# Two neighbouring gate/up chunks as one product whose first half of K takes seven block products, in both feed-forwards of a macaron decoder block

## The chip, the cores and the metric

The kernel runs on one core of a Trainium2 chip. Time is device microseconds of one execution, as the median of several runs. TensorE is PE in the profile (PEld its weight loads), VectorE is DVE, ScalarE is ACT, GpSimd is POOL, and SP is the engine whose queue issues nearly all DMAs.

## The reference

The block reads 256 tokens of 1024 features (float32). Only its first and last stage, the two feed-forwards, are touched:

```python
def swiglu(x, w_gate, w_up, w_down):
    return (jax.nn.silu(x @ w_gate) * (x @ w_up)) @ w_down
...
h = h + 0.5 * swiglu(rmsnorm(h, ffn1_norm[l]), ffn1_w_gate[l], ffn1_w_up[l], ffn1_w_down[l])
...   # mixing: attention and chunked spatial gating, gated merge, output projection
h = h + 0.5 * swiglu(rmsnorm(h, ffn2_norm[l]), ffn2_w_gate[l], ffn2_w_up[l], ffn2_w_down[l])
return rmsnorm(h, final_norm)
```

`w_gate` and `w_up` are 1024 x 2816, `w_down` is 2816 x 1024.

## The kernel before, in words

**Three passes.** Each float32 product is made of fp32r products: every operand is kept as a high part (a rounded copy) and a low part (what the rounding left). `mm3` multiplies one 128-row block of K with 512 output columns in three matmuls (lines 240 to 242): high by high, high by low, low by high. A 128-token block of the activations is the stationary operand, 512 weight columns are the moving one.

**Chunks and units.** Gate and up are computed in eleven chunks of 256 hidden columns; a chunk has 256 gate and 256 up columns, that is 512 output columns for two token blocks and eight blocks of K, 8 x 2 x 3 = 48 matmuls into two PSUM banks (`chunk`). The weights of a chunk come in two units, one for each half of K, of four blocks each. A unit is fetched in two halves of 512 KB (`fetch_to`, ring `raw` of 7 buffers, SP queue). `split` turns each 128x1024 half into its parts: ACT writes the high one (line 245), DVE subtracts for the low one (line 247). Units live in the ring `w` of 5 buffers. `unit(i, ahead)` writes units up to `ahead` past the one that PE is about to use; in most of the feed-forwards `ahead` is DEEP = 4, so the next unit can be written as soon as PE has left the unit five places back.

**After a chunk** `Hidden.glu` scales by the token factors: ACT takes the SiLU of the gate columns out of PSUM (line 505), DVE multiplies with the up columns (507) and transposes 32x32 blocks (508). `Hidden.move` carries the result through DRAM (`f1way`, `f1back`) to the layout with hidden features on partitions, `f1h`.

**Seven products.** The down projections already take eight of their 22 blocks of K in pairs by a seven-product scheme (`seven`): a 2x2 arrangement of token blocks by K blocks times a 2x2 arrangement of K blocks by column halves in seven block products instead of eight. Four products use forms of the token side (four sums of 128x128 blocks, lines 543 to 546, then `split`), and four use sums of weight blocks, made on DVE by four adds of 128x512 (`quarters`, lines 194 to 197, tile `sum`, two buffers). The weights of such a pair are two units in the ring: "single" (three 512-column blocks used as they are) and "sums" (four made ones). Of the seven, three go straight into output banks, and four into shared banks (1, 5, 6 and 7), which `settle_seven` adds up at the end.

**Order.** PE and SP run in the order of the source. DVE and ACT are put in order by a scheduler, apart from the stretches under `in_order()`, which hold the start of the first feed-forward and all from its down projection to the second chunk of the second one. PSUM has eight banks. `n` is the normalised input in its two parts, `f` the chunks' banks, `accdown` and `acch` the banks of the two down projections, `h` the residual between the feed-forwards.

Of the kernel before, what the change touches and what calls it, by code (L numbers as in the profile page):

```python
# [43 lines left out]
REST = [k for k in range(FB) if k // 2 not in SEVEN]  # L44
PLAIN = len(REST) // 2
WARM = 17


@with_exitstack
def block_kernel(ctx, tc, t, out):  # L50
# [56 lines left out]
    def add_units(name, n):  # L107
        first = len(units)
        units.extend((name, i) for i in range(n))
        return first  # L110

    f1 = add_units("f1", 2 * NC)


    f1d = []
# [11 lines left out]
    mb = len(units)  # L129
    units.extend([("bg", 0), ("ba", 0), ("bg", 1), ("ba", 1)])  # L130
    mo = add_units("out", 4)
    f2 = add_units("f2", 2 * NC)

# [228 lines left out]
            banks[key] = bank(f"acc{name}" + "_".join(map(str, key)))  # L364
        mm3(banks[key], st, w, first, last)

    def seven(name, at, i, tokens_of, acc, shared, ahead=DEEP):


        a, b, d = tokens_of(2 * i, 0), tokens_of(2 * i + 1, 0), tokens_of(2 * i + 1, 1)  # L370
        last = i == SEVEN[-1]

        def of(w, n):
            return w[:, n, 0, :], w[:, n, 1, :]

        def form(n):
            return tuple(hidden.forms[i][:, n, two, :] for two in range(2))

        w = unit(at, ahead)
        product(shared, name, (1,), a, of(w, 0), last)  # L380
        product(acc, name, (0, 0), b, of(w, 1), False)
        product(acc, name, (0, 512), form(3), of(w, 2), False)
        w = unit(at + 1, ahead)
        product(shared, name, (5,), form(0), of(w, 0), last)
        product(shared, name, (7,), form(1), of(w, 1), last)
        product(shared, name, (6,), form(2), of(w, 2), last)
        product(acc, name, (1, 0), d, of(w, 3), False)
# [24 lines left out]
    def down(at, part_of, scale, hh, name, done, cuts, behind):  # L412

        acc, shared = {}, {}
        K = 2 * len(at)
        near = K - 4

        def add(ps, j, c0, n):
            sl = slice(c0, c0 + n)
            nc.vector.scalar_tensor_tensor(hh[:, j, sl], ps, scale, hh[:, j, sl], op0=ALU.mult, op1=ALU.add)

        def tokens_of(k, j):
            return tuple(p[:, j * P:(j + 1) * P] for p in part_of(k))

        def ends(j, c0, k):
            return k == (K - 1 if (c0, 512) in cuts[j] else near - 1)

        for i in range(len(at) - 2):
            if i in SEVEN:
                seven(name, at[i], i, tokens_of, acc, shared)
                if i == SEVEN[-1]:
                    settle_seven(name, shared, scale, hh)()
            else:
                w = unit(at[i], DEEP)
                for kk in range(2):
                    for j in range(NT):
                        for c0, n in HALVES:  # L440
                            product(acc, name, (j, c0), tokens_of(2 * i + kk, j),
                                    tuple(w[:, kk, two, c0:c0 + n] for two in range(2)), ends(j, c0, 2 * i + kk))
            for then in behind[i:i + 1]:
                then()
        for j in range(NT):
            for c0, n in HALVES:
                if (c0, n) not in cuts[j]:
                    add(acc[j, c0], j, c0, n)
        for j in range(NT):
            for hf, (c0, n) in enumerate(cuts[j]):  # L450
                whole = (c0, n) in HALVES
                ps = acc[j, c0] if whole else bank(f"end{name}{j}{c0}")[:, :n]
# [37 lines left out]
    class Hidden:  # L490
# [45 lines left out]
        def form(self, p, e, to):  # L536

            def of(j, k):
                return self.back[p][:, 4 * j:4 * j + 4, 64 * e + 32 * k:64 * e + 32 * (k + 1)]

            f = tmp.tile([P, 4, P], F32, tag="form", name=f"{self.name}form{p}{e}", bufs=1)
            of_f = [f[:, n].rearrange("p (q c) -> p q c", c=32) for n in range(4)]
            nc.vector.tensor_sub(of_f[0], of(1, 1), of(1, 0))
            nc.vector.tensor_sub(of_f[1], of(0, 0), of(1, 0))
            nc.vector.scalar_tensor_tensor(of_f[2], of_f[0], -1.0, of(0, 0), op0=ALU.mult, op1=ALU.subtract)
            nc.vector.tensor_add(of_f[3], of_f[2], of(0, 1))
            split(to[:, :, 0, :], to[:, :, 1, :], f)
            self.forms[2 * p + e] = to

        def settle(self, p):  # L550
# [65 lines left out]
    with in_order():  # L616
        x = inputs_of(front[:, KB:KB + KB * ROW])
        split_to(f1 + 3)
        for pair in range(KB // 2):
            square(x[:, 2 * pair:2 * pair + 2, :], pair, "1", "nC")  # L620
        split_half()
        token_sums("1")
        split_half()
        sum_parts("1")
        sums.append(chunk(f1, nT, "f1", 1))
        rs = token_factors("1")
        sums.append(chunk(f1, nT, "f1", 2))
        hidden = Hidden("f1")
        for c in range(2):
            hidden.glu(c, sums[c], rs)  # L630

    ht1 = act.tile([P, NT, D], F32, tag="nD", name="ht1")
    for j in range(NT):
        nc.sync.dma_start(ht1[:, j, :], t["by_tokens"][j * P:(j + 1) * P, :])
    for c in range(2, NC):
        if c > 2:
            sums.append(chunk(f1, nT, "f1", c, ahead=DEEP))
            hidden.form_behind(c, ("h", "nC"))
            for moved in (1, 2, 3) if c == 3 else (c,):
                hidden.move(moved)  # L640
        hidden.glu(c, sums[c], rs)
# [18 lines left out]
    with in_order():  # L660
# [30 lines left out]
        for n, (at, s) in enumerate(f1d):  # L691

            ahead = 1 if len(SEVEN) * 2 - 2 <= n < len(SEVEN) * 2 else DEEP
            if s is not None:
                seven("down1", at, SEVEN[s], tokens_of, acc, shared, ahead)
                if s == len(SEVEN) - 1:
                    settled.append(settle_seven("down1", shared, 0.5, ht1))
            else:
                w = unit(at, ahead)
                slots = range(4 * units[at][1], 4 * units[at][1] + 4)  # L700
                ends = slots[-1] == 2 * len(REST) - 1
                for slot, j in [(x, j) for j in range(NT) for x in slots] if ends else [(x, j) for x in slots for j in range(NT)]:
                    f, b = divmod(slot, len(REST))
                    last = b == len(REST) - 1
                    product(acc, "down1", (j, f * 512), tokens_of(REST[b], j),
                            tuple(w[:, slot % 4, two, :] for two in range(2)), last)
                    if last:
                        add(f, j, acc[j, f * 512])
                        if j == NT - 1:
                            from_way(h[:, f], h_way[f])  # L710
                            if f == 0:
                                settled.pop()()
            for then in rest[n:n + 1]:
                then()
            if n == len(f1d) - 3:
                norm_parts(0)
# [259 lines left out]
                nc.vector.transpose(squares32[:, b].rearrange("p (f c) r -> p f c r", f=2),  # L976
                                    h[:, :, b, :].rearrange("p f (c r) -> p f c r", r=32))
    hd = dram.tile([S, D], F32, name="hd")
    ht = act.tile([P, NT, D], F32, tag="nA", name="ht")
    for c in range(2, NC):  # L980
        ps = chunk(f2, nT3, "f2", c, ahead=DEEP)
        if c == 2:
            hidden.move(1)
        hidden.form_behind(c, ("h", "nB"))
        hidden.move(c)
        hidden.glu(c, ps, rs)
        if c == 3:
            for a in range(4):
                nc.sync.dma_start(hd[:, a * UC:(a + 1) * UC].rearrange("(b c) n -> c b n", c=32),
                                  squares32[32 * a:32 * a + 32].rearrange("p b k r -> p b (k r)"))  # L990
        elif c == 5:
            for j in range(NT):
                nc.sync.dma_start(ht[:, j, :], hd[j * P:(j + 1) * P, :])
        elif c == 7:
            gain4 = act.tile([P, D], F32, tag="ws", name="gain4")
            nc.sync.dma_start(gain4, t["final_norm"].to_broadcast([P, D]))

# [43 lines left out]
def _packed(inputs):  # L1041
# [33 lines left out]
    def chunks(w):  # L1075
# [6 lines left out]
    first = np.concatenate([columns(a["ffn1_norm"][0][order], KB), by_k.reshape(P, -1)], 1)  # L1082
    got = {
        "first": first,
        "f1": chunks(pairs[1]), "f2": chunks(pairs[2]),
        "by_tokens": a["x"][0][:, turned],
        "f1s": rows(down1)[list(SEVEN)],
        "f1d": down1.reshape(FB, P, 2, 512)[REST].transpose(2, 0, 1, 3).reshape(PLAIN, 4, P, 512).transpose(0, 2, 1, 3),
# [32 lines left out]
```

## Time and profile before

| | |
|---|---|
| median of 3 runs | 519.33 us (518.91 to 519.96) |
| the profiled execution: its own time, and its span | 519.43 us, 517.7 us |
| mean granted PE clock | 0.996 |
| PE, PEld, DVE, ACT, POOL busy | 509.5, 424.0, 403.9, 281.1, 12.0 us |
| PE instructions, DVE, ACT | 2377, 585, 395 |
| HBM read and written | 113.26 and 13.11 MB, 244 GB/s over the span |

The span runs from the first to the last instruction; the execution's own time has 1.7 us more around it. First feed-forward: gate and up chunks from 6 to 126 us, then its down projection to 185 us. Second one: chunks from 334 to 454 us, down projection to 510 us. A matmul's row says 389 ns, but that is from its start to its modelled end, and the next one starts before it. So rates are read from start times.

### The profile page before, as it was taken

Reading aid. Unit: us, or ns where it says so; the run is one execution under the profiler, and the core shown is the slowest. Engines: PE = TensorE matmul, PEld = TensorE weight load, DVE = VectorE, ACT = ScalarE, POOL = GpSimd, SP = SyncE. Lnnn points to the kernel's source line nnn. Section 1 sums busy time; section 2 is a strip of 40 time slices with the busy share of each in tenths; the row PEclk is TensorE's granted clock in tenths of the full one; section 3 lists DMA queues with packets and bytes.
Section 4 is the critical chain, followed back from the end, with each engine's and each line's share of the span. In section 5 each row is a group of like instructions: output and inputs, shape, how many; then the busy total and the mean of one; then the engine's idle time right before and its main releaser. Section 6 shows DMA issues by size and latency. Waiting matters only on the chain.

```text
span 517.7 us, 6795 instructions
## 1 busy us (share of the span) xinstructions
PE 509.5 (98%) x2377; PEld 424.0 (82%) x2377; DVE 403.9 (78%) x585; ACT 281.1 (54%) x395; POOL 12.0 (2%) x25
## 2 busy tenths in 40 slices
PE   8999999999999999999999999999999999999995
PEld 6888888888888888888888898888888888888884
DVE  5896685888798965579977776988876666899864
ACT  6775445455474736667565613668535544466702
POOL 0010000000000010000000000001000000000002
PEclk9999999999999999999999999999999999999998
DMA  8999499867576886796899665839989879389302
GB/s 312 359 335 392 142 316 329 263 181 256 163 226 221 270 311 214 186 325 239 204 361 333 240 184 161 304 98 307 310 255 325 249 282 282 91 282 282 124 0 82
DMA packets 63921, 126.81 MB, mean 245 GB/s; under 512 B 11664, under 2 KB 36752, under 8 KB 63760
## 3 DMA queue, kind: packets, MB, share of 16 engines
q1 hardware_dynamic: 63600, 126.06, 74.1%
q8 instruction: 18, 0.29, 0.2%
q10 hardware_dynamic: 288, 0.33, 0.2%
q14 instruction: 15, 0.12, 0.1%
HBM read 113.26 MB, written 13.11 MB: 244 GB/s over the span
## 4 chain that ended last, share of the span: by engine, by line
PE 94%; DMA 2%; DVE 1%; issue 1%; SPq 1%; ACT 0%; POOLq 0%; DVEq 0%; POOL 0%; ACTq 0%
PE f L242 15%; PE f L241 15%; PE f L240 15%; PE accdown L242 4%; PE accdown L241 4%; PE accdown L240 4%; PE acch L242 4%; PE acch L241 4%; PE acch L240 3%; PE acc L214 3%; PE g L241 3%; PE g L242 3%; PE g L240 3%; DMA raw<-in_gate 1%; PE acc L219 1%; DMA front<-in_first 1%
## 5 line engine op out<-in xcount | busy, mean ns | idle before, releaser
L247 DVE TENSOR_TENSOR w<-raw,w 128x1024 fp32r<-128x1024 f32 (+1 forms) x180 | 207.2, 1194 | 36.6 <-ACT w L245 36.1
L245 ACT CAST w<-raw 128x1024 fp32r<-128x1024 f32 (+1 forms) x180 | 176.3, 1030 | 52.1 <-PE f L242 38.5
L242 PE MATMUL f<-w,n 128*128 128x512 f32 x336 | 130.7, 389 | 0.0
L240 PE MATMUL f<-w,n 128*128 128x512 f32 x336 | 130.7, 389 | 0.0
L241 PE MATMUL f<-w,n 128*128 128x512 f32 x336 | 130.7, 389 | 0.0
L241 PEld LDWEIGHTS f<-w,n 128*128 128x128 f32 x336 | 63.1, 188 | 13.2
L240 PEld LDWEIGHTS f<-w,n 128*128 128x128 f32 x336 | 63.1, 188 | 13.1
L242 PEld LDWEIGHTS f<-w,n 128*128 128x128 f32 x336 | 63.1, 188 | 13.0
L505 ACT ACTIVATE f2s<-f,rstd 128x256 f32<-128x256 f32 x22 | 10.3, 474 | 30.1 <-PE f L242 30.1
L240 PE MATMUL accdown<-w,f1h 128*128 128x512 f32 x68 | 26.5, 389 | 0.0
L241 PE MATMUL accdown<-w,f1h 128*128 128x512 f32 x68 | 26.5, 389 | 0.0
L242 PE MATMUL accdown<-w,f1h 128*128 128x512 f32 x68 | 26.5, 389 | 0.0
L245 ACT CAST w<-sum 128x1024 fp32r<-128x1024 f32 x16 | 16.7, 1053 | 16.9 <-DVE sum L195 13.1
L240 PE MATMUL g<-w,n 128*128 128x512 f32 x64 | 24.9, 389 | 0.0
L241 PE MATMUL g<-w,n 128*128 128x512 f32 x64 | 24.9, 389 | 0.0
L240 PE MATMUL acch<-w,f2h 128*128 128x512 f32 x64 | 24.9, 389 | 0.0
L241 PE MATMUL acch<-w,f2h 128*128 128x512 f32 x64 | 24.9, 389 | 0.0
L242 PE MATMUL acch<-w,f2h 128*128 128x512 f32 x64 | 24.9, 389 | 0.0
L242 PE MATMUL g<-w,n 128*128 128x512 f32 x64 | 24.9, 389 | 0.0
L507 DVE SCALAR_TENSOR_TENSOR f2a<-f,rstd,f2s 128x256 f32<-128x256 f32 x22 | 10.2, 474 | 13.5 <-ACT f2s L505 13.5
L247 DVE TENSOR_TENSOR w<-sum,w 128x1024 fp32r<-128x1024 f32 x16 | 19.3, 1216 | 1.2 <-ACT w L245 1.2
L505 ACT ACTIVATE f1s<-f,rstd 128x256 f32<-128x256 f32 x22 | 10.2, 473 | 16.1 <-PE f L242 15.7
(225 smaller groups left out, 768.4 us busy)
## 6 DMA issues: line engine op xcount, KB each, us to landing
raw<-in_f SPq DMA_DIRECT2D x84, 512.0 KB, 6.2
raw<-in_f2d SPq DMA_DIRECT2D x22, 512.0 KB, 6.5
raw<-in_gate SPq DMA_DIRECT2D x16, 512.0 KB, 5.9
raw<-in_f1d SPq DMA_DIRECT2D x14, 512.0 KB, 5.0
raw<-in_f1s SPq DMA_DIRECT2D x8, 512.0 KB, 4.8
raw<-in_out SPq DMA_DIRECT2D x8, 512.0 KB, 5.4
f1way<-f1t SPq DMA_DIRECT2D x11, 256.0 KB, 5.6
f2way<-f2t SPq DMA_DIRECT2D x11, 256.0 KB, 6.1
```

The costliest lines, as they stand in the source:

```text
L214: nc.tensor.matmul(ps, st, both.rearrange("p two n -> p (two n)"), start=first, stop=last)
L219: nc.tensor.matmul(ps[:, n:], st, both[:, 0, :], start=False, stop=False)
L240: nc.tensor.matmul(ps, sh, mh, start=first, stop=False)
L241: nc.tensor.matmul(ps, sh, ml, start=False, stop=False)
L242: nc.tensor.matmul(ps, sl, mh, start=False, stop=last)
L245: nc.scalar.copy(hi, src)
L247: nc.vector.tensor_sub(lo, src, hi.bitcast(F32))
L505: nc.scalar.activation(sg, ps[j][:, :CH], AF.Silu, scale=rs[j])
L507: nc.vector.scalar_tensor_tensor(a, ps[j][:, CH:], rs[j], sg, op0=ALU.mult, op1=ALU.mult)
```

## The change

Chunks 6 and 7 of each feed-forward become one product of 1024 columns (2 x 512). Its first four blocks of K are taken in two pairs by `seven`, 2 x 7 x 3 = 42 matmuls where 2 x 8 x 3 = 48 stood; the last four blocks are multiplied as before (`rest`), first for chunk 6, then for chunk 7. Their weights are regrouped on the host: four units for the seven-product part (single, sums, single, sums) and one unit for each chunk's second half of K. The fetched bytes are the same.

```diff
+PAIR = {"f1": 6, "f2": 6}
...
+    def add_chunks(name):
+        c = PAIR[name]
+        first = add_units(name, 2 * c)
+        units.extend((f"{name}s2", i, what) for i in range(2) for what in ("single", "sums"))
+        units.extend((name, i) for i in range(2 * c, 2 * NC - 2))
+        return first
...
+    def make_forms(of, to, name):
+        f = tmp.tile([P, 4, P], F32, tag="form", name=name, bufs=1)
+        of_f = [f[:, n].rearrange("p (q c) -> p q c", c=32) for n in range(4)]
+        nc.vector.tensor_sub(of_f[0], of(1, 1), of(1, 0))
+        nc.vector.tensor_sub(of_f[1], of(0, 0), of(1, 0))
+        nc.vector.scalar_tensor_tensor(of_f[2], of_f[0], -1.0, of(0, 0), op0=ALU.mult, op1=ALU.subtract)
+        nc.vector.tensor_add(of_f[3], of_f[2], of(0, 1))
+        split(to[:, :, 0, :], to[:, :, 1, :], f)
+
+    def chunk_pair(name, at, nT, forms, ahead):
+        acc, shared = {}, {}
...
+        for i in range(2):
+            seven(name, at + 2 * i, i, tokens_of, acc, shared, forms[:, i], i == 1, ahead)
+        p1, p5, p6, p7 = (shared[n,] for n in (1, 5, 6, 7))
+        to = [sump.tile([P, NT, 512], F32, tag="sum", name=f"{name}{e}") for e in range(2)]
+        (c00, c10), (c01, c11) = ([x[:, j] for j in range(NT)] for x in to)
+        nc.scalar.copy(c00, p1)
+        nc.vector.tensor_add(c01, p6, c00)
+        nc.vector.tensor_add(c10, p7, c01)
+        nc.vector.tensor_add(c11, p5, c10)
+        nc.vector.tensor_add(c01, p5, c01)
+
+        def rest(e):
+            w = unit(at + 4 + e, ahead)
+            for k in range(4):
+                for j in range(NT):
+                    product(acc, name, (j, 512 * e), tokens_of(4 + k, j), (w[:, k, 0, :], w[:, k, 1, :]), k == 3)
+            for j in range(NT):
+                x = to[e][:, j]
+                (nc.vector.tensor_sub if e else nc.vector.tensor_add)(x, acc[j, 512 * e], x)
+            return [to[e][:, j] for j in range(NT)]
+        return rest
...
+        normed1 = sump.tile([P, 4, S // 32, 32], F32, tag="sum", name="normed1")
+        for k in range(4):
+            nc.scalar.activation(normed1[:, k].rearrange("p q c -> p (q c)"), x[:, k], AF.Identity, scale=front[:, k:k + 1])
...
-            sums.append(chunk(f1, nT, "f1", c, ahead=DEEP))
+            sums.append(chunk_of("f1", f1, nT, c, pair_forms))
+            if c == 3:
+                for i in range(2):
+                    make_forms(lambda j, k: normed1[:, 2 * i + k, 4 * j:4 * j + 4, :], pair_forms[:, i], f"pair1form{i}")
...
-    ht = act.tile([P, NT, D], F32, tag="nA", name="ht")
+    pair_forms = act.tile([P, 2, 4, 2, P], F32R, tag="nA", name="pairforms")
...
-        elif c == 5:
+        elif c == PAIR["f2"] + 2:
+            ht = act.tile([P, NT, D], F32, tag="nA", name="ht")
...
-        elif c == 7:
+        elif c == PAIR["f2"] + 3:
```

`chunk_of` sends c = 6 and 7 to the two calls of `rest`, c = 6 after `chunk_pair`; the second feed-forward gets the same lines as the first, with `normed` from `h`. The forms need the first four normalised blocks in plain float32, hence `normed1` and `normed`. In the second feed-forward the buffer `nA` first holds the forms, so the load of the residual `ht` moves from chunk 5 to chunk 8 and that of `gain4` from chunk 7 to chunk 9.

What the scheduler makes of it at three places follows. First DVE in the first feed-forward, while PE is in chunk 1. The tile `sq` holds the squares for the token factors, `sqp` their split sum, `w_270` the second unit of chunk 1, `w_285` (`w_290` after) the first of chunk 2. Before:

```order
L247 TENSOR_TENSOR w_270<-raw_0_192,w_270 128x2x512
L279 TENSOR_TENSOR sq_265<-sq_265 128x1024
L279 TENSOR_TENSOR sq_265<-sq_265 128x512
L279 TENSOR_TENSOR sq_265<-sq_265 128x256
L247 TENSOR_TENSOR w_270<-raw_1_194,w_270 128x2x512
L247 TENSOR_TENSOR sqp_280<-sq_265,sqp_280 128x256
L247 TENSOR_TENSOR w_285<-raw_0_196,w_285 128x2x512
```

After:

```order
L256 TENSOR_TENSOR w_270<-raw_0_192,w_270 128x2x512
L288 TENSOR_TENSOR sq_265<-sq_265 128x1024
L400 TENSOR_TENSOR pair1form_560<-normed_280 128x128
L288 TENSOR_TENSOR sq_265<-sq_265 128x512
L401 TENSOR_TENSOR pair1form_560<-normed_280 128x128
L288 TENSOR_TENSOR sq_265<-sq_265 128x256
L256 TENSOR_TENSOR w_270<-raw_1_194,w_270 128x2x512
L256 TENSOR_TENSOR sqp_285<-sq_265,sqp_285 128x256
L402 SCALAR_TENSOR_TENSOR pair1form_560<-pair1form_560,normed_280 128x128
L256 TENSOR_TENSOR w_290<-raw_0_196,w_290 128x2x512
```

The sums of the first forms now stand among the token sums, ahead of the second half of `w_270`.

Second, DVE at the end of the output projection, where `h` and the parts `n` for the second feed-forward are made and PE is about to begin its chunk 0; `w_2970` (`w_3021` after) is the first unit of chunk 1, `w_3013` (`w_3064`) its second. Before:

```order
L311 SCALAR_TENSOR_TENSOR n_2779<-h,cols,n_2779 128x256 x2
L247 TENSOR_TENSOR w_2970<-raw_0_2795,w_2970 128x2x512
L247 TENSOR_TENSOR w_2970<-raw_1_2836,w_2970 128x2x512
L279 TENSOR_TENSOR sq_2943<-sq_2943 128x1024
L279 TENSOR_TENSOR sq_2943<-sq_2943 128x512
L279 TENSOR_TENSOR sq_2943<-sq_2943 128x256
L247 TENSOR_TENSOR sqp_3007<-sq_2943,sqp_3007 128x256
L247 TENSOR_TENSOR w_3013<-raw_0_2840,w_3013 128x2x512
```

After:

```order
L401 TENSOR_TENSOR pairform_3414<-normed 128x128
L402 SCALAR_TENSOR_TENSOR pairform_3414<-pairform_3414,normed 128x128
L320 SCALAR_TENSOR_TENSOR n_2830<-h,cols,n_2830 128x256
L256 TENSOR_TENSOR w_3021<-raw_0_2846,w_3021 128x2x512
L256 TENSOR_TENSOR w_3021<-raw_1_2887,w_3021 128x2x512
L288 TENSOR_TENSOR sq_2994<-sq_2994 128x1024
L403 TENSOR_TENSOR pairform_3414<-pairform_3414,normed 128x128
L288 TENSOR_TENSOR sq_2994<-sq_2994 128x512
L288 TENSOR_TENSOR sq_2994<-sq_2994 128x256
L256 TENSOR_TENSOR pairforms<-pairform_3414,pairforms 128x4x128
L256 TENSOR_TENSOR sqp_3058<-sq_2994,sqp_3058 128x256
L256 TENSOR_TENSOR w_3064<-raw_0_2891,w_3064 128x2x512
```

All ten DVE instructions of the two forms stand in this stretch, six of them among the rows of `h` and `n` above these, ahead of the units that PE needs next.

Third, DVE at the pair of the second feed-forward, after PE's seven products: `f2p` are the sums of the shared banks `accf2p`, `w_3675` and `w_3693` the units of chunk 8.

```order
L256 TENSOR_TENSOR w_3675<-raw_0_3546,w_3675 128x2x512
L420 TENSOR_TENSOR f2p_3715<-accf2p_3667,f2p_3714 128x512
L256 TENSOR_TENSOR w_3675<-raw_1_3581,w_3675 128x2x512
L421 TENSOR_TENSOR f2p_3714<-accf2p_3663,f2p_3715 128x512
L256 TENSOR_TENSOR w_3693<-raw_0_3585,w_3693 128x2x512
L422 TENSOR_TENSOR f2p_3715<-accf2p_3659,f2p_3714 128x512
L423 TENSOR_TENSOR f2p_3715<-accf2p_3659,f2p_3715 128x512
L432 TENSOR_TENSOR f2p_3714<-accf2p_0_3642,f2p_3714 128x512
L432 TENSOR_TENSOR f2p_3714<-accf2p_0_3671,f2p_3714 128x512
L565 SCALAR_TENSOR_TENSOR f2a_3769<-f2p_3714,rstd_3180,f2s_3767 128x256
```

The same place before, where the two units of chunk 8 are `w_3559` and `w_3592`:

```order
L247 TENSOR_TENSOR w_3559<-raw_0_3388,w_3559 128x2x512
L247 TENSOR_TENSOR w_3559<-raw_1_3417,w_3559 128x2x512
L508 STREAM_TRANSPOSE f2t_3544<-f2a_3547 128x256
L508 STREAM_TRANSPOSE f2t_3544<-f2a_3552 128x256
L247 TENSOR_TENSOR w_3592<-raw_0_3421,w_3592 128x2x512
L507 SCALAR_TENSOR_TENSOR f2a_3638<-f_60_3557,rstd_3129,f2s_3636 128x256
L507 SCALAR_TENSOR_TENSOR f2a_3643<-f_61_3558,rstd_3129,f2s_3641 128x256
L247 TENSOR_TENSOR w_3592<-raw_1_3474,w_3592 128x2x512
```

Chunk 8's units now stand with the adds that wait for PE's shared banks and for the end of `rest`.

More of the change, by code (lines that the diff above doesn't have):

```diff
@@ L110, in add_units @@
         return first
-    f1 = add_units("f1", 2 * NC)
+    def add_chunks(name):
[4 more added lines that the diff above has]
+        return first
+    f1 = add_chunks("f1")
     f1d = []
@@ L131, in block_kernel @@
     mo = add_units("out", 4)
-    f2 = add_units("f2", 2 * NC)
+    f2 = add_chunks("f2")
     f2d = []
@@ L365, in product, with seven @@
         mm3(banks[key], st, w, first, last)
-    def seven(name, at, i, tokens_of, acc, shared, ahead=DEEP):
+    def seven(name, at, i, tokens_of, acc, shared, forms, last, ahead=DEEP):
         a, b, d = tokens_of(2 * i, 0), tokens_of(2 * i + 1, 0), tokens_of(2 * i + 1, 1)
-        last = i == SEVEN[-1]
         def of(w, n):
@@ L376, in form @@
         def form(n):
-            return tuple(hidden.forms[i][:, n, two, :] for two in range(2))
+            return tuple(forms[:, n, two, :] for two in range(2))
         w = unit(at, ahead)
@@ L387, in seven, with tokens_of, chunk_of @@
         product(acc, name, (1, 0), d, of(w, 3), False)
+    def make_forms(of, to, name):
[8 more added lines that the diff above has]
+        acc, shared = {}, {}
+        def tokens_of(k, j):
+            return tuple(p[:, j * P:(j + 1) * P] for p in block_of(nT, k))
+        for i in range(2):
[18 more added lines that the diff above has]
+        return rest
+    pending = {}
+    def chunk_of(name, first, nT, c, forms):
+        at = c - PAIR[name]
+        if at == 0:
+            pending[name] = chunk_pair(name + "p", first + 2 * c, nT, forms, DEEP)
+        if at in (0, 1):
+            return pending[name](at)
+        return chunk(first + 2 * (at > 0), nT, name, c, ahead=DEEP)
     def settle_seven(name, shared, scale, hh):
@@ L432, in down @@
             if i in SEVEN:
-                seven(name, at[i], i, tokens_of, acc, shared)
+                seven(name, at[i], i, tokens_of, acc, shared, hidden.forms[i], i == SEVEN[-1])
                 if i == SEVEN[-1]:
@@ L539, in of @@
                 return self.back[p][:, 4 * j:4 * j + 4, 64 * e + 32 * k:64 * e + 32 * (k + 1)]
[L541 to L547, printed above, removed]
+            make_forms(of, to, f"{self.name}form{p}{e}")
             self.forms[2 * p + e] = to
@@ L630, in block_kernel @@
             hidden.glu(c, sums[c], rs)
+    pair_forms = act.tile([P, 2, 4, 2, P], F32R, tag="nC", name="pairforms1")
     ht1 = act.tile([P, NT, D], F32, tag="nD", name="ht1")
@@ L694, in block_kernel @@
             if s is not None:
-                seven("down1", at, SEVEN[s], tokens_of, acc, shared, ahead)
+                seven("down1", at, SEVEN[s], tokens_of, acc, shared, hidden.forms[SEVEN[s]], s == len(SEVEN) - 1, ahead)
                 if s == len(SEVEN) - 1:
@@ L978, in block_kernel @@
     hd = dram.tile([S, D], F32, name="hd")
-    ht = act.tile([P, NT, D], F32, tag="nA", name="ht")
+    pair_forms = act.tile([P, 2, 4, 2, P], F32R, tag="nA", name="pairforms")
     for c in range(2, NC):
-        ps = chunk(f2, nT3, "f2", c, ahead=DEEP)
+        ps = chunk_of("f2", f2, nT3, c, pair_forms)
         if c == 2:
             hidden.move(1)
+            normed = sump.tile([P, 4, S // 32, 32], F32, tag="sum", name="normed")
+            for k in range(4):
+                nc.scalar.activation(normed[:, k], h_block(k), AF.Identity, scale=gain3[:, k:k + 1])
+        if c == 3:
+            for i in range(2):
+                make_forms(lambda j, k: normed[:, 2 * i + k, 4 * j:4 * j + 4, :], pair_forms[:, i], f"pairform{i}")
         hidden.form_behind(c, ("h", "nB"))
@@ L1084, in _packed @@
         "first": first,
-        "f1": chunks(pairs[1]), "f2": chunks(pairs[2]),
+        **{f"f{n}": np.delete(chunks(pairs[n]), [2 * PAIR[f"f{n}"], 2 * PAIR[f"f{n}"] + 2], 0) for n in (1, 2)},
+        **{f"f{n}s2": rows(pairs[n][:D // 2, PAIR[f"f{n}"]:][:, :2].reshape(D // 2, -1)) for n in (1, 2)},
         "by_tokens": a["x"][0][:, turned],
```

## The prediction

> **What bounds the kernel now.** I read the page's busy shares and chain first, then the waits of PE and of the weight casts, then ACT's rows in order of time for PE's pace.
>
> ```profile
> PE 509.5 (98%) x2377; PEld 424.0 (82%) x2377; DVE 403.9 (78%) x585; ACT 281.1 (54%) x395; POOL 12.0 (2%) x25
> PE 94%; DMA 2%; DVE 1%; issue 1%; SPq 1%; ACT 0%; POOLq 0%; DVEq 0%; POOL 0%; ACTq 0%
> ```
>
> ```profile
> PE warm L101 <- DVE zeros L98: 1.2, 1, 1.2
> PE f L610 <- ACT n L586: 0.9, 1, 0.9
> ```
>
> ```profile
> ACT w L245 <- PE f L242: 41.1, 16, 3.4
> DVE w L247 <- ACT w L245: 37.3, 33, 4.0
> ```
>
> The chain that ends last is PE for 94%. PE's own waits are these two, both before its first real matmul: in both feed-forwards it never waits for weights. The other way round, the casts wait 41.1 us for PE to leave a buffer of the ring: weights run as far ahead as the five buffers allow. So what takes matmuls from PE shortens the kernel by those matmuls, until something else is late.
>
> PE's pace comes from two chunk ends. Each f1s row starts as its chunk's last matmul ends; the releaser says so:
>
> ```profile
> 49.63 0.48 ACT L505 ACTIVATE f1s<-f,rstd 128x256 f32<-128x256 f32 x1 [2.75 <-PE f L242]
> ...
> 114.97 0.47 ACT L505 ACTIVATE f1s<-f,rstd 128x256 f32<-128x256 f32 x1 [2.29 <-PE f L242]
> ```
>
> These are the ends of chunks 3 and 9, six chunks of 48 matmuls: 65.34 / 288 = 0.2269 us a matmul, 10.89 us a chunk. (A row's 389 ns would give too much, as the rows overlap.)
>
> **What it removes.** Per feed-forward 96 matmuls become 42 + 48 = 90. Twelve fewer: 12 x 0.2269 = 2.72 us. The new products have the shape of the old and change the stationary block as often. The Trainium skill, "TensorE: Matmul & The Clock Gate", section "Back-to-back issue gap", gives 512 columns 216 ns alone and 131 ns in a long stream; by these the term would be an estimated 2.6 or 1.6 us. The rows say 226.9 ns in a long stream, so the trace agrees with neither and its own pace is used.
>
> **What it adds on DVE and ACT.** Prices are distances between starts of neighbouring rows:
>
> ```profile
> 23.87 6.90 DVE L247 TENSOR_TENSOR w<-raw,w 128x1024 fp32r<-128x1024 f32 x6
> ...
> 90.62 0.28 DVE L543 TENSOR_TENSOR f1form<-f1back 128x128 f32<-128x128 f32 x1
> 90.82 0.29 DVE L544 TENSOR_TENSOR f1form<-f1back 128x128 f32<-128x128 f32 x1
> ...
> 92.69 0.68 DVE L247 TENSOR_TENSOR f1forms<-f1form,f1forms 128x512 fp32r<-128x512 f32 x1
> 93.29 1.22 DVE L247 TENSOR_TENSOR w<-raw,w 128x1024 fp32r<-128x1024 f32 x1
> ...
> 437.13 0.68 DVE L194 TENSOR_TENSOR sum<-raw 128x512 f32<-128x512 f32 x1
> 437.74 0.68 DVE L195 TENSOR_TENSOR sum<-raw,raw 128x512 f32<-128x512 f32 x1
> ```
>
> ```profile
> 11.31 0.51 ACT L586 ACTIVATE n<-front 128x256 fp32r<-128x256 f32 x1
> 11.72 0.61 ACT L598 CAST w<-front 128x512 fp32r<-128x512 f32 x1
> ```
>
> DVE per feed-forward: the first half of K has 4 halves of 1024 to split before, and 2 of 512 and 6 of 1024 after: 2 x 0.60 + 2 x 1.15 = 3.5. Weight sums 8 x 0.61 = 4.9. Adds of the shared banks 4 x 0.61 and onto the results 4 x 0.61 = 4.9. Two forms, each 4 x 0.20 + 0.60 = 2.8. Together 16.1 us. ACT: four scalings of 0.41 (the L586 row is the same kind), casts of 2 x 0.5 and 2 x 1.0 for weights and 2 x 0.5 for forms, one copy from PSUM of some 0.6: 6.2 us. SiLU and product now read SBUF, not PSUM; I cost that at nothing, bounded by the whole of the 0.48 us rows. None of this is on PE, so its cost is zero as long as units arrive in time. The room, chunks 4 to 7 of each feed-forward:
>
> ```profile
> 50.10:61.00 10.90, 10.90 (x50) 9.01 (x49) 6.53 (x10) 4.38 (x6) 0.00 (x0) 1.00 0.37 122
> 61.00:71.90 10.90, 10.90 (x50) 9.03 (x49) 7.97 (x14) 5.81 (x9) 0.00 (x0) 1.00 0.95 292
> 71.90:82.70 10.80, 10.80 (x49) 8.97 (x48) 7.42 (x9) 5.66 (x8) 0.00 (x0) 1.00 0.96 291
> 82.70:93.60 10.90, 10.90 (x49) 9.03 (x49) 8.07 (x14) 6.34 (x9) 0.00 (x0) 1.00 0.88 315
> ```
>
> ```profile
> 378.20:389.10 10.90, 10.90 (x50) 9.03 (x49) 6.46 (x10) 4.85 (x6) 0.00 (x0) 1.00 0.95 263
> 389.10:400.00 10.90, 10.90 (x49) 9.03 (x49) 7.63 (x14) 5.37 (x7) 0.00 (x0) 1.00 0.99 332
> 400.00:410.80 10.80, 10.80 (x49) 8.93 (x48) 6.35 (x9) 4.84 (x6) 0.00 (x0) 1.00 0.74 200
> 410.80:421.70 10.90, 10.90 (x50) 9.03 (x49) 6.39 (x9) 4.84 (x6) 0.00 (x0) 1.00 1.03 402
> ```
>
> Columns: span, then PE, PEld, DVE, ACT, POOL busy, granted clock, DMA. First feed-forward: DVE idles 43.5 - 30.0 = 13.5 us, 12.1 after the stretch shrinks by 1.4; 14.7 us arrive (16.1 less 1.4 of the first form, done earlier). 2.6 us slip into chunk 8. That is allowed: a unit can be written from when PE leaves the one five places back, four units or about 20 us early. Second: idle 16.7, 15.3 after shrinking; 16.1 - 2.8 = 13.3 arrive. It fits.
>
> **Where DVE's order puts PE behind something.** Halves of chunk 8's units now stand behind adds that wait for the end of the seven products or of the first `rest`. PE needs each of these halves 60 matmuls or 13.6 us after the event that its place in the queue waits for (48 + 12, and 24 + 36); some 6 us of DVE work stand between. Hidden. The eight banks of the pair are all in use; the seventh product needs the bank of chunk 5's first token block:
>
> ```profile
> 71.96 0.48 DVE L507 SCALAR_TENSOR_TENSOR f1a<-f,rstd,f1s 128x256 f32<-128x256 f32 x1 [0.34 <-ACT f1s L505]
> ```
>
> Chunk 5 ends at 49.63 + 21.8 = 71.4, the bank is free at 72.4, its product comes 18 matmuls on, at 75.5: 3 us spare.
>
> **The tight places** are the two starts, where the forms are squeezed in. First feed-forward:
>
> ```profile
> 17.82 1.99 ACT L245 CAST w<-raw 128x1024 fp32r<-128x1024 f32 x2
> ...
> 20.04 2.41 DVE L279 TENSOR_TENSOR sq<-sq 128x1024 f32<-128x1024 f32 x3
> 22.36 1.22 DVE L247 TENSOR_TENSOR w<-raw,w 128x1024 fp32r<-128x1024 f32 x1
> ...
> 25.39 0.39 PE L240 MATMUL f<-w,n 128*128 128x512 f32 x1
> ```
>
> The last half unit of chunk 1 is done at 23.6 and its low part is used 36 matmuls into the chunk, at 25.6. Two form sums (0.4) and the wait for four scalings (ACT free at 19.8, done at 21.45; DVE at 21.24) make it 0.6 later: 1.4 us spare. Second feed-forward, the stretch just ahead of its chunk 0 and then the rows:
>
> ```profile
> 328.80:334.40 5.60, 5.60 (x34) 4.89 (x33) 5.46 (x13) 2.05 (x4) 0.00 (x0) 1.00 0.95 347
> ```
>
> ```profile
> 334.27 0.39 PE L240 MATMUL f<-w,n 128*128 128x512 f32 x1
> ...
> 339.77 0.48 DVE L311 SCALAR_TENSOR_TENSOR n<-h,cols,n 128x256 fp32r<-128x256 f32 x1 [0.18 <-ACT n L307]
> 340.18 2.35 DVE L247 TENSOR_TENSOR w<-raw,w 128x1024 fp32r<-128x1024 f32 x2
> ...
> 346.33 6.91 DVE L247 TENSOR_TENSOR w<-raw,w 128x1024 fp32r<-128x1024 f32 x6 [0.53 <-ACT w L245]
> ...
> 350.61 0.40 PE L289 MATMUL sums<-sqp,ones 128*128 128x512 f32 x1
> ```
>
> The last `n` is ready at 340.25 and used 44 matmuls in, at 344.3; seven form sums and a low part (2.0) go ahead of it: 2 us spare. Chunk 1's first unit: ready 341.4, used 345.2, again 2.0 later, 1.8 spare. Its second: ready 347.5, used 351.1; all 2.8 us of forms ahead, some of it in the gaps there: 0.8 to 2 spare. No stall, narrowly.
>
> **Moves on SP.** The loads of `ht` and `gain4` go behind those of some more weights; first use of `ht` in the down projection:
>
> ```profile
> 406.09 0.88 SPq L993 DMA_DIRECT2D ht<-hd x2
> ```
>
> ```profile
> L397 DVE SCALAR_TENSOR_TENSOR ht<-acch,ht x1: 686/686/686, 490.7 to 490.7; 128x512 f32<-128x512 f32 x1
> ```
>
> Three chunks (33 us) later is still 50 us early. `gain4`, two chunks later, is used after that. Both are cost at nothing; the weights behind them on SP come 0.9 us later and have the ring's lead. Fetched bytes stay the same.
>
> **Sum.** 519.43 - 2.72 = 516.71 for the profiled execution; it stands 0.1 above the median, which makes 516.6.
>
> **Rivals.**
> *A, the starts are late.* If forms' ACT and DVE work adds up one after the other instead of side by side (each form sum waiting for its scaling, each low part for its cast), the second start gets 4 x 0.41 + 2 x 0.5 + 2.8 = 5.4 us, less some 3.5 of room: 2.0 of stall; the first 4 x 0.41 + 0.8 = 2.4 against 2.0: 0.4. So 516.7 to 519.0. For it: DVE is busy 5.46 of 5.60 us ahead of the second start. Against: most of the order interleaves them.
>
> *B, DVE takes PE's place (slower).* Place: units of the pair. About ten new hand-overs per feed-forward (cast to low part, sum to cast, with two `sum` buffers). The 33 waits above average 1.1 us. At 1.5 us each, 15 us go on top: in the first feed-forward 2.6 + 15, less 10 that the fourth unit of the pair has in hand (it may be written from 24 + 30 matmuls ahead, 12.3 us, less 2.3 for its writing), 7.6 of stall; in the second 15 - 2.0 - 10 = 3. That is 527. It decides from 1.0 us a hand-over, where the stalls reach 2.7. Against: those waits are mostly idleness, DVE waiting for a cast that waits for PE's buffer (the 41.1 us above), and the down projections take such pairs with PE never waiting. The Trainium skill, "Perfetto Trace Analysis", section "Identifying the Most-Contended Engine", judges PE by its weight loads and calls the engine with the highest occupancy the one to relieve. By it DVE, at an estimated 436 of 515 us or 85%, would pass PEld's 82%, and this change would be wrong. The trace so far speaks against that: PE issues without a gap at 82%.
>
> *C, DMA sets the pace.* Then the same bytes take the same time: 519.3.
>
> ```profile
> raw<-in_f SPq DMA_DIRECT2D x84, 512.0 KB, 6.2
> ```
>
> ```profile
> ACT w L245 <- DMA raw<-in_f: 4.7, 8, 1.5
> ```
>
> For it: DMA is near 1.0 in several windows. Against: its 4.7 us of waits end in ACT, none in PE.
>
> **Chances.** Forecast 0.80 (516.2 to 517.1), A 0.13, B 0.04, C 0.03. About 0.2%, 1.0 us, is what a measurement can tell here (the three runs lie 1.05 apart). Faster by more, below 518.3: the forecast and a good third of A, 0.85. Within: the rest of A, and C, 0.11. Slower 0.04. The range takes in the forecast and A up to its middle: 516.0 to 518.3.
>
> **What would show it.** PE x2365; DVE x645 and busy some 436 us; still no PE wait inside the chunks; chunks 6 and 7 ending 90 x 0.2269 = 20.4 us after chunk 5 instead of 21.8, twice; all later rows 1.4, then 2.7 us earlier. A wait of PE on `w` or `n` near 25 or 345 us is A; one near 80 or 405 us is B; DMA as a releaser of PE is C. An unchanged pace with a longer span would break the argument as a whole.

## The result, and the profile after

The changed kernel takes 516.47 us (median of 6 runs, 516.21 to 517.18) against 519.4 us (518.91 to 519.96) for the kernel before on the same chip: ratio 0.9946, 95% interval 0.9934 to 0.9958, that is 2.8 us less. The profiled execution took 516.24 us, its span is 514.5 us, its mean clock 0.996.

The page's busy shares and the chain, after:

```profile
PE 506.8 (98%) x2365; PEld 421.8 (82%) x2365; DVE 434.3 (84%) x645; ACT 293.8 (57%) x417; POOL 12.0 (2%) x25
PE 94%; DMA 2%; DVE 1%; issue 1%; SPq 0%; ACT 0%; POOLq 0%; DVEq 0%; POOL 0%; ACTq 0%
```

Twelve matmuls are gone, DVE has 60 instructions and 30.4 us more, and PE still carries 94% of the chain. Next the waits, first PE's own (both of them), then those of the casts (cast and releaser: us in total, times, longest):

```profile
PE warm L102 <- DVE zeros L99: 1.2, 1, 1.2
PE v L249 <- DVE mixed L830: 0.4, 1, 0.4
```

```profile
ACT w L254 <- PE f L251: 24.7, 11, 3.5
ACT w L254 <- DVE sum L204: 19.4, 6, 4.9
DVE w L256 <- ACT w L254: 15.9, 19, 1.8
```

PE waits nowhere in either feed-forward (`v` belongs to the mixing between them). The casts waited 41.1 us for PE before and wait 24.7 now: the weights still run ahead as far as the ring lets them, but with less idle time. The ends of chunks 5 and 8 of the first feed-forward, by ACT's rows:

```profile
70.61 0.48 ACT L563 ACTIVATE f1s<-f,rstd 128x256 f32<-128x256 f32 x1 [2.29 <-PE f L251]
101.83 0.47 ACT L563 ACTIVATE f1s<-f,rstd 128x256 f32<-128x256 f32 x1 [2.76 <-PE f L251]
```

31.22 us for 90 + 48 matmuls; the kernel before had these ends at 71.45 and 104.03, 32.58 us for 144. The difference is 1.36 us, six matmuls at 0.2269. The second feed-forward shows 31.27 against 32.64, 1.37 less. So 2.73 us of the gain are in the two places where the matmuls were taken out. The span fell by 3.2; the rest is that PE's first real matmul came 0.9 earlier (5.02 instead of 5.91, a load that landed sooner; in the profiles of the runs below it comes at 5.0 to 5.6, with or without the change), less the 0.4 at `v`. Now 20.4 us in each pair, which begin 1.3 and 0.4 us after the chunk ahead of it has ended:

```profile
71.90:92.30 20.40, 20.40 (x91) 16.89 (x90) 20.26 (x30) 15.04 (x18) 0.00 (x0) 1.00 0.78 244
397.90:418.30 20.40, 20.40 (x91) 16.89 (x91) 18.01 (x28) 11.55 (x16) 0.00 (x0) 1.00 0.71 223
```

After the span stand the busy times of PE, PEld, DVE, ACT and POOL. DVE is busy 20.26 of 20.40 us in the first feed-forward: it has almost no idle time left there, and PE is nevertheless busy throughout.

### The profile page after: what moved, and what is told of

It reads as the page before. It is cut to its first block, busy times and chain, and to the rows that moved or that the text cites. A ratio compares the mean times of both kernels' runs of the same rounds, so it can differ in the third digit from the quotient of the medians.

```text
span 514.5 us, 6844 instructions
## 1 busy us (share of the span) xinstructions
PE 506.8 (98%) x2365; PEld 421.8 (82%) x2365; DVE 434.3 (84%) x645; ACT 293.8 (57%) x417; POOL 12.0 (2%) x25
## 2 busy tenths in 40 slices
DMA packets 63922, 126.82 MB, mean 246 GB/s; under 512 B 11664, under 2 KB 36752, under 8 KB 63760
## 4 chain that ended last, share of the span: by engine, by line
PE 94%; DMA 2%; DVE 1%; issue 1%; SPq 0%; ACT 0%; POOLq 0%; DVEq 0%; POOL 0%; ACTq 0%
PE f L251 12%; PE f L250 12%; PE f L249 12%; PE accdown L251 4%; PE accdown L250 4%; PE accdown L249 4%; PE acch L251 4%; PE acch L250 4%; PE acch L249 4%; PE acc L223 3%; PE g L250 3%; PE g L251 3%; PE g L249 3%; PE acc L228 1%; DMA raw<-in_gate 1%; PE accf2p L251 1%
## 5 line engine op out<-in xcount | busy, mean ns | idle before, releaser
L254 ACT CAST w<-raw 128x1024 fp32r<-128x1024 f32 (+1 forms) x180 | 174.0, 1019 | 28.0 <-PE f L251 13.1
L251 PE MATMUL f<-w,n 128*128 128x512 f32 x272 | 105.8, 389 | 0.0
L249 PE MATMUL f<-w,n 128*128 128x512 f32 x272 | 105.8, 389 | 0.0
L250 PE MATMUL f<-w,n 128*128 128x512 f32 x272 | 105.8, 389 | 0.0
L250 PEld LDWEIGHTS f<-w,n 128*128 128x128 f32 x272 | 51.1, 188 | 10.7
L249 PEld LDWEIGHTS f<-w,n 128*128 128x128 f32 x272 | 51.1, 188 | 10.6
L251 PEld LDWEIGHTS f<-w,n 128*128 128x128 f32 x272 | 51.0, 188 | 10.5
L254 ACT CAST w<-sum 128x1024 fp32r<-128x1024 f32 x24 | 25.1, 1052 | 33.4 <-DVE sum L204 19.4
L256 DVE TENSOR_TENSOR w<-sum,w 128x1024 fp32r<-128x1024 f32 x24 | 29.0, 1219 | 1.0 <-ACT w L254 0.9
L223 PE MATMUL acc<-mg,w 128*128 128x512 f32 x64 | 17.0, 393 | 0.0
L563 ACT ACTIVATE f1s<-f,rstd 128x256 f32<-128x256 f32 x18 | 8.4, 471 | 14.7 <-PE f L251 14.5
L563 ACT ACTIVATE f2s<-f,rstd 128x256 f32<-128x256 f32 x18 | 8.5, 475 | 14.3 <-PE f L251 11.9
```

Of the source, the lines that this page charges most:

```text
L223: nc.tensor.matmul(ps, st, both.rearrange("p two n -> p (two n)"), start=first, stop=last)
L249: nc.tensor.matmul(ps, sh, mh, start=first, stop=False)
L250: nc.tensor.matmul(ps, sh, ml, start=False, stop=False)
L251: nc.tensor.matmul(ps, sl, mh, start=False, stop=last)
L254: nc.scalar.copy(hi, src)
L256: nc.vector.tensor_sub(lo, src, hi.bitcast(F32))
```

## The experiments

Two theories. **Matmuls**: PE alone sets the time, so the gain is the twelve matmuls and all the added work on DVE and ACT is hidden by idle time and by the ring's lead. **Cover** (the rivals A and B): the hidden work is close to its limit or partly over it, at the starts or in the pairs.

**The matmuls given back.** The first matmul into each of six banks of the pair is issued twice (the second overwrites the first), so PE does as many as before and everything else stays:

```diff
             banks[key] = bank(f"acc{name}" + "_".join(map(str, key)))
+            if name.endswith("p") and key != (1, 0) and key != (1, 512):
+                nc.tensor.matmul(banks[key], st[0], w[0], start=True, stop=True)
```

> The changed kernel with twelve matmuls given back, six in each feed-forward: the first matmul into each of six banks of the pair is issued twice. All added DVE and ACT work and all new hand-overs stay. Theory (the gain is nothing but the twelve matmuls at PE's pace): the whole gain goes, 519.2 to 519.6 us, within 0.1% of the kernel before. Rival (the gain comes in part from elsewhere: fewer waits of the casts, loads landing earlier, the order): a part stays, 517.5 to 518.5. Rival (DVE's work is near its limit and costs something that the fewer matmuls outweigh): 520 or more.

518.43 us against 518.61, ratio 0.9998 (0.9989 to 1.0007). Its page:

```profile
PE 509.3 (99%) x2377; PEld 424.2 (82%) x2377; DVE 434.8 (84%) x645; ACT 293.7 (57%) x417; POOL 12.0 (2%) x25
```

With PE's 2377 instructions and DVE's 645 the time is that of the kernel before, within a tenth of a per cent. The expected times were written for a kernel before of 519.4 us; it takes 518.61 here, so the ratio decides, and not that 518.43 lies in the range of the first rival. The gain is the twelve matmuls; 30 us of DVE work and 12 us of ACT work cost nothing that can be measured (the interval is some 0.5 us to either side).

**One feed-forward at a time.** The changed kernel with a list of pairs for each feed-forward:

```diff
-PAIR = {"f1": 6, "f2": 6}
+PAIRS = {'f1': [6], 'f2': []}     # the other run: 'f1': [], 'f2': [6]
```

> The pair in the first feed-forward alone; the second one as before. Theory: six matmuls less, 1.36 us, so 518.0 us. Rival (a late start in the first feed-forward, or waits in its pair, where DVE is fullest, eat part): 518.3 to 519.4, and a PE wait near 25 or 80 us. Rival (one feed-forward carries the whole gain): 516.6 or 519.4.

> The pair in the second feed-forward alone; the first one as before. Theory: 1.36 us less, 518.0 us, and the two gains add up to that of the whole change. Rival (the second start is late): up to 2 us of stall, 518.4 to 520.0, with a PE wait near 345 us.

First alone: 517.43 us against 518.61, ratio 0.9977 (0.9968 to 0.9986). Second alone: 517.28, the same ratio and interval. Each is 1.2 us (0.7 to 1.7), which holds the 1.36 of six matmuls; together 2.4, against 2.8 for the whole change, within the intervals. Neither carries the gain alone.

**The second start made late.** In the output projection, where DVE prepares `n` and the units of chunk 1, the last low part is computed four, and in another run eleven, times more:

```diff
+        for _ in range(4 if name == "3" else 0):     # 11 in the other run
+            low_part(nT, KB - 1, gain)
         low_part(nT, KB - 1, gain)
```

> The changed kernel with the last low part of n (DVE, ahead of the second feed-forward) computed four times more, 4 x 0.40 = 1.6 us of DVE work in the tightest place; the scheduler also puts 0.8 us of the forms in front of it. Theory: the trace after shows the last n ready at 339.57 us and first used at 342.40, 2.8 spare; 2.4 us fit, so no wait of PE and the same time, 516.5 us. Rival (the start is already at its limit, so every microsecond in DVE's queue is a microsecond of time): 1.6 to 2.4 us more, 518.1 to 518.9, with a PE wait near 342 us.

> As the run with four more low parts, with eleven: 11 x 0.40 = 4.4 us. With four, the first half unit of chunk 1's second unit came 0.3 us late (PE's only loss), so 2.8 us more of DVE work should cost 2.8 us more. Theory (what goes past the spare time is paid one to one): 516.5 + 0.3 + 2.8 = 519.6 us, 0.99 to 1.002 of the kernel before, most of it in one PE wait on n near 342 us. Rival (later cover takes a part back, or the scheduler's order shields it): 517 to 518.5.

With four: 516.5 us against 518.61, ratio 0.9959 (0.9946 to 0.9973). The changed kernel's 0.9946 (0.9934 to 0.9958) overlaps with it, so the times show no loss; the rows show a small one. For comparison the changed kernel, DVE and then PE at this place:

```profile
339.09 0.48 DVE L320 SCALAR_TENSOR_TENSOR n<-h,cols,n 128x256 fp32r<-128x256 f32 x1
...
345.73 4.63 DVE L256 TENSOR_TENSOR w<-raw,w 128x1024 fp32r<-128x1024 f32 x4 [0.53 <-ACT w L254]
```

```profile
342.40 0.39 PE L251 MATMUL f<-w,n 128*128 128x512 f32 x1
...
349.22 0.39 PE L250 MATMUL f<-w,n 128*128 128x512 f32 x1
```

The last `n` is ready at 339.57 and first used at 342.40; the low part of chunk 1's second unit is ready at 345.73 + 1.2 = 346.9 and used at 349.22: 2.3 us spare at the tighter of the two. With four more low parts the same rows are:

```profile
348.24 2.36 DVE L256 TENSOR_TENSOR w<-raw,w 128x1024 fp32r<-128x1024 f32 x2 [0.52 <-ACT w L254]
```

```profile
348.99 0.40 PE L249 MATMUL f<-w,n 128*128 128x512 f32 x1
349.52 0.50 PE L250 MATMUL f<-w,n 128*128 128x512 f32 x1
```

DVE is 2.5 us later, and PE starts 0.53 us after its neighbour where 0.23 is its pace: 0.3 us of stall. So the start has 2.2 us to spare, and the point where it begins to cost has been hit.

With eleven: 523.57 us against 519.62, ratio 1.0075 (1.0056 to 1.0094), where 519.6 was expected. PE's rows around its wait, and the granted clock after it (the third number from the end, 0.54):

```profile
342.29 0.39 PE L250 MATMUL f<-w,n 128*128 128x512 f32 x1
346.92 0.53 PE L251 MATMUL f<-w,n 128*128 128x512 f32 x1 [4.24 <-DVE n L320]
...
347.67 0.63 PE L250 MATMUL f<-w,n 128*128 128x512 f32 x1
...
350.65 0.40 PE L251 MATMUL f<-w,n 128*128 128x512 f32 x1
```

```profile
347.00:350.00 3.00, 3.00 (x8) 2.37 (x9) 3.00 (x3) 0.00 (x0) 0.00 (x0) 0.54 0.28 75
```

Two things made it dearer. The repeated low parts cost some 0.5 us each and not 0.40 (eight of them took 4.12 us), so the wait is 4.2 us. And behind it nine matmuls, 346.92 to 350.65, take 3.73 us where nine at 0.2269 take 2.04: the clock was granted at about a half. 4.24 + 1.7 = 5.9 of the 6.2 us by which this span is longer than the changed kernel's.

**The weight sums on POOL.** Only the pairs' own sums move:

```diff
+                adder = nc.gpsimd if units[i][0] in ("f1s2", "f2s2") else nc.vector
-                nc.vector.tensor_add(first[:, 0], a, b)
+                adder.tensor_add(first[:, 0], a, b)
...
```

> The changed kernel with the weight sums of the two pairs (8 adds of 128x512 each) on POOL instead of DVE: 16 x 0.61 = 9.8 us less on DVE, which falls from 434 to some 424 us, at or below PEld's 422; POOL takes 16 x 1.04 = 17 us. Theory (PE's matmuls set the time, DVE is covered): the same time, 516.5 us, plus or minus 0.5. Rival (DVE, at 84% the busiest after PE and above PEld's 82%, is a bound that relief moves): 1 to 5 us faster. Rival (POOL's adds are slower one by one, 4.2 us a unit instead of 2.4, and come in the way of DVE): a wait of PE in the pairs, near 80 or 405 us, 517.5 or more.

517.36 us against 519.38, ratio 0.9962 (0.9949 to 0.9975); the changed kernel's was 0.9946 (0.9934 to 0.9958). No gain on top, as the theory said, but DVE was not relieved either:

```profile
PE 506.7 (98%) x2365; PEld 421.9 (82%) x2365; DVE 437.2 (85%) x629; ACT 294.0 (57%) x417; POOL 40.1 (8%) x41
```

16 instructions fewer and 3 us more busy. POOL's rows, and DVE's in the same stretch:

```profile
387.14 1.34 POOL L212 TENSOR_TENSOR sum<-raw,raw 128x512 f32<-128x512 f32 x1
388.44 1.33 POOL L213 TENSOR_TENSOR sum<-sum,raw 128x512 f32<-128x512 f32 x1
389.85 2.36 POOL L214 TENSOR_TENSOR sum<-sum,raw 128x512 f32<-128x512 f32 x1
```

```profile
387.25 1.37 DVE L409 TENSOR_TENSOR f2form<-f2back 128x128 f32<-128x128 f32 x1
388.55 1.37 DVE L410 SCALAR_TENSOR_TENSOR f2form<-f2form,f2back 128x128 f32<-128x128 f32 x1
389.84 1.21 DVE L264 TENSOR_TENSOR f2h<-f2back,f2h 128x1024 fp32r<-128x1024 f32 x1
```

These adds of 128x128 take 0.28 us elsewhere; here each begins during a POOL add and ends just after it. DVE's split of 128x1024, which begins just ahead of a POOL add, takes its usual 1.21 us, and then the POOL add takes 2.36 us instead of 1.3. The two take turns. So this run does not show what a freer DVE would bring; it shows that moving these sums to POOL does not free DVE.

**Two pairs.** Chunks 4+5 and 8+9, from the same forms, in the second feed-forward; then in both; then in both with the sums on POOL:

```diff
-PAIRS = {'f1': [6], 'f2': [6]}
+PAIRS = {'f1': [6], 'f2': [4, 8]}     # the others: 'f1': [4, 8], 'f2': [4, 8]
```

> The second feed-forward takes two pairs, chunks 4+5 and 8+9, from the same forms; the first keeps one. Six matmuls less: 1.36 us. A second pair adds 3.5 + 4.9 + 4.9 = 13.3 us of DVE work where DVE idles 11.7 us in chunks 3 to 10. Theory (DVE's idle time over the feed-forward plus the ring's lead is the room): it just fits, 515.1 us, or misses by 1 to 2 us, 516 to 517. Rival (DVE's load never matters): 515.1 exactly, with no wait of PE. Rival (the room is gone with one pair): 518 or more.

> Two pairs in both feed-forwards: twelve matmuls less than the changed kernel, 2.72 us. In the first, 13.3 us of DVE work meet 7.0 us of idle time in chunks 3 to 10. Theory: 513.8 us plus a stall in the first feed-forward of 2 to 6 us, 516 to 520, with PE waiting for w there and DVE at 99% or more over several chunks. Rival (matmuls alone count): 513.8.

> Two pairs in both feed-forwards, with all their weight sums on POOL (32 adds of 1.04 us). DVE gets 13.3 - 9.8 = 3.5 us more per feed-forward than the changed kernel, inside the 7.0 and 11.7 us of idle time. Theory: no stall, 513.8 us, the fastest of all. Rival (POOL's adds are too slow in a row or slow DVE down): a stall, 515 to 518.

All three are slower than the kernel before, which takes 519.38 us here: 528.59 us, ratio 1.018 (1.0166 to 1.0194); 540.99 us, 1.0405 (1.0378 to 1.0432); 540.85 us, 1.0395 (1.036 to 1.043). The theory's times were too low by 12 to 27 us. For the first of the three the rival that expected 518 us or more (the room is gone with one pair) was right in its range; for the other two every range was too low by 20 us or more. The kernel with two pairs in the second feed-forward, PE's waits first:

```profile
PE accf2p L256 <- DVE f2a L572: 6.4, 1, 6.4
PE accf2p L256 <- ACT pairforms L261: 1.6, 1, 1.6
PE accf2p L257 <- DVE w L263: 1.3, 1, 1.3
```

```profile
420.00:431.00 11.00, 7.96 (x36) 6.25 (x34) 11.00 (x21) 6.13 (x8) 0.00 (x0) 1.00 0.57 171
431.00:442.00 11.00, 7.65 (x25) 6.17 (x26) 11.00 (x14) 7.70 (x9) 0.00 (x0) 0.69 0.83 215
```

DVE is busy 11.00 of 11.00 us in both, and PE waits. For what, the rows tell, ACT's first, then DVE's and PE's:

```profile
423.29 0.47 ACT L570 ACTIVATE f2s<-f,rstd 128x256 f32<-128x256 f32 x1
```

```profile
433.71 0.88 DVE L572 SCALAR_TENSOR_TENSOR f2a<-f,rstd,f2s 128x256 f32<-128x256 f32 x2
```

```profile
427.57 0.39 PE L258 MATMUL accf2p<-w,pairforms 128*128 128x512 f32 x1
434.35 0.77 PE L256 MATMUL accf2p<-w,n 128*128 128x512 f32 x1 [6.39 <-DVE f2a L572]
...
438.75 0.42 PE L257 MATMUL accf2p<-w,pairforms 128*128 128x512 f32 x1
```

PE has done six of the first seven products of the pair and waits for the bank of the seventh. That bank holds the chunk before the pair until DVE's product with the up columns (`f2a`) has read it. The SiLU that this product needs (`f2s`) is ready at 423.8, but the product runs at 433.71: it stands in DVE's queue behind weight sums and splits, and behind forms for the down projection. It costs 6.4 us, and then ten matmuls at 0.44 us instead of 0.227, 2.1 more. The span is 12.7 us longer although six matmuls, 1.36 us, are gone, so 14.1 us have to be explained. These 8.5 are three fifths of it; the late forms and units of the pair at chunk 4 (3.5 us of waits) are another quarter.

With two pairs in both feed-forwards, the first feed-forward has a wait of this kind at its first pair (the profiled executions of the last two kernels, 537.81 and 534.99 us, are the fastest of their six). PE's wait, the SiLU, DVE's product, and the busy times of the stretch:

```profile
PE accf1p L256 <- DVE f1a L572: 7.0, 1, 7.0
```

```profile
49.41 0.47 ACT L570 ACTIVATE f1s<-f,rstd 128x256 f32<-128x256 f32 x1 [3.29 <-PE f L258]
```

```profile
60.52 0.83 DVE L572 SCALAR_TENSOR_TENSOR f1a<-f,rstd,f1s 128x256 f32<-128x256 f32 x2
```

```profile
50.00:61.00 11.00, 4.07 (x18) 3.02 (x17) 9.37 (x12) 6.86 (x8) 0.00 (x0) 0.86 0.50 158
```

The SiLU is ready at 49.9 us and the product runs at 60.52, yet DVE is busy only 9.37 of these 11.00 us. The rest it idles, because instructions ahead of the product wait for casts and, for 0.7 us, for a DMA that still reads `f1t`. So what holds PE is the product's place in DVE's queue, and not only how much DVE has to do. Two things stay open: no run puts this product further ahead in the queue, and none has a single pair at chunk 4 or 8, so the price of a second pair is not told apart from the price of these places.

With the sums on POOL this wait is 8.6 us; DVE is busy 460.2 us, and was 460.8 without POOL's help.

**A ring of four.** Four weight buffers instead of five, in the kernel before and in the changed one:

```diff
-RING = 5
+RING = 4
```

> The kernel before with four weight buffers in the ring instead of five, so weights are made at most three units ahead instead of four. It is the base for the next run. Its casts waited 41 us for PE to leave a buffer; a quarter less lead should cost little: 519.4 to 522 us.

> The changed kernel with four weight buffers. Theory (the ring's lead is the cover, and the pair in the first feed-forward needs about 2.6 us of it, of 16 us that three units give): still hidden, 2.7 us less than the kernel before with four buffers, give or take 1. Rival (the pair uses up the lead, DVE being 20.26 of 20.4 us busy beside it in the first feed-forward): one unit less of lead, 5.4 us, turns into stalls in the first feed-forward, and the change then costs time, 0 to 6 us more than the kernel before with four buffers, with PE waiting for w or for banks near 75 to 95 us.

526.09 us (ratio 1.0125, 1.0104 to 1.0146) and 525.76 us (1.0122, 1.0095 to 1.0149). With four buffers both lose more than expected, and the change brings 0.3 us instead of 2.8: less than the theory said, and no loss as the rival had it. The times of one kernel spread over 2.6 and 3.7 us here, so this 0.3 is uncertain by some 1.7 us (an estimate from that spread). What follows is read from one profiled execution of each, 525.44 and 525.10 us. The ends of chunks 5 and 8 in the first feed-forward, the kernel before and then the changed one:

```profile
71.13 0.47 ACT L505 ACTIVATE f1s<-f,rstd 128x256 f32<-128x256 f32 x1 [1.35 <-PE f L242]
...
103.71 0.47 ACT L505 ACTIVATE f1s<-f,rstd 128x256 f32<-128x256 f32 x1 [2.75 <-PE f L242]
```

```profile
70.99 0.47 ACT L563 ACTIVATE f1s<-f,rstd 128x256 f32<-128x256 f32 x1 [2.73 <-PE f L251]
...
102.21 0.47 ACT L563 ACTIVATE f1s<-f,rstd 128x256 f32<-128x256 f32 x1 [2.75 <-PE f L251]
```

32.58 and 31.22: the pair saves its 1.36 us with four buffers too, and DVE's full stretch is still covered. What is lost is lost elsewhere, in PE's waits, before and then after (a third wait, 2.1 us on `g` in the mixing, is the same in both):

```profile
PE f L241 <- DVE w L247: 1.8, 2, 1.4
PE v L240 <- DVE mixed L771: 1.4, 1, 1.4
```

```profile
PE f L250 <- DVE w L256: 3.0, 2, 2.6
PE v L249 <- DVE mixed L830: 2.7, 1, 2.7
```

The waits on `f` are at the second start (345 us): DVE, with the forms' work in its queue, gets to that unit at 344.73 us instead of 343.81, and PE waits 1.2 us more in all. That is the place of rival A. The wait on `v` in the mixing is 1.3 longer. It also differs between runs with a ring of five (none before, 0.4 after, 0.9 with the sums on POOL), and why is open. Together they make the 2.5 us that are missing.

## Why the prediction was right, point by point

- **Bound and pace.** PE was the bound before and after. The pace taken from chunk ends, 0.2269 us, gave 1.36 us for each feed-forward; the rows show 1.36 and 1.37, and the matmuls put back took the gain away.
- **The sum.** 516.6 us forecast, 516.47 measured. The profiled execution was to be 516.71 and was 516.24: the 0.9 us of an earlier start, less the 0.4 at `v`, are not the change's doing. Part of the closeness is therefore chance.
- **Work added on DVE and ACT, costed at nothing.** DVE was put at x645 and 436 us, and has x645 and 434.3. ACT was put at 6.2 us for each feed-forward, 12.4 in all, and got 12.7. The first feed-forward was to have no idle time left and to slip into chunk 8; DVE is busy 20.26 of 20.40 us in the pair, and 10.70 of 10.80 in chunk 8.
- **The tight places.** The second start was said to have 0.8 to 2 us left at chunk 1's second unit; the late starts put it at 2.2. The bank of the seventh product was given 3 us spare. In the trace it is free at 71.6 (71.11 + 0.48, DVE's `f1a`) and used at 75.1, 3.5 us. In the two-pair kernels the longest waits are at this place; late forms and units cost 3.5 us there.
- **Rival A** did not occur, but its place was right: the second start is 2.2 us away from costing anything, and with a ring of four it costs 1.2 us.
- **Rival B** did not occur with one pair, and does with two. Its price was set on hand-overs of 1.5 us in the units of the pair. Those from cast to low part got cheaper (DVE's waits for casts went from 37.3 to 15.9 us in all, 0.8 each); those from sum to cast got dearer (ACT's waits for sums went from 14.4 to 21.8), but no wait of PE came of them. What stalls with two pairs is PE's bank: the product that frees it stands far back in DVE's queue, and a stall of 6 us then costs 8 since the clock drops. The working names this bank, with 3 us to spare, but rival B was not priced on it, nor on the clock. The Trainium skill, "Perfetto Trace Analysis", section "Identifying the Most-Contended Engine", would have named DVE, 84% against PEld's 82%, as the engine to relieve. By whole-span occupancy that did not hold here: with the matmuls put back, DVE had 30 us more to do than in the kernel before and the time was the same, and with DVE's load unchanged twelve matmuls alone made the difference of 2.8 us. Taken by stretch, DVE at 11.00 of 11.00 us does name the engine behind the wait of 6.4 us; at the wait of 7.0 us it was busy 9.37 of 11.00.
- **Rival C** did not occur: the same bytes (126.82 MB) in less time.

## What to carry to other kernels

Take the gain of removed matmuls from the distance of chunk ends, not from rows, and cover for the added work from the idle time of each stretch and from how early its results may be made; here that gave the time to within 0.2 us, in part by chance. The same reckoning missed the two-pair kernels by 12 us and more. So before using the same trick twice, look for the shared resource that another engine's queue releases (here a PSUM bank behind DVE's weight work), and for what stands ahead of the release in that queue: one pair at chunk 6 costs nothing that can be measured, and with pairs at chunks 4 and 8 of the second feed-forward in its place the kernel is 12 us slower. To learn how far one is from that edge, put known work into the tight place until the engine that sets the time waits.

## What the runs showed of the hardware

- **A long wait of PE costs some 2 us on top of its length.** Waits of 4.2, 6.4, 7.0 and 8.6 us were each followed by eight to ten matmuls at about 0.43 us, at a granted clock near 0.5, for 3.5 to 4.4 us. Waits of 1.3, 1.6, 2.6 and 2.9 us were not: the matmuls behind them go on at 0.23 to 0.24. The Trainium skill, "TensorE: Matmul & The Clock Gate", section "What's actually happening", has the clock halve after an idle window of about 3.4 us and come back after a busy one; the trace agrees, with the change between 2.9 and 4.2 us here.
- **POOL and DVE hold each other up.** A DVE add of two SBUF inputs that begins during a POOL add of 128x512 lasts to its end: 1.37 us for 128x128, where 0.28 is usual. A POOL add that begins during a DVE split waits in its turn: 2.36 us instead of 1.3. The Trainium skill, "GPSIMD Engine Reference", section "1. Specifications", says that its SBUF interface is shared with VectorE and that instructions with two SBUF inputs contend; the trace agrees.
